# The value product of attention with its high and low part in one matmul

## Chip, cores and metric

One core of a Trainium2 chip. The metric is the device time of one execution in microseconds: 647.28 as the median of 3 runs of the kernel before (647.21 to 647.37). Inputs and output are float32.

## What is computed

One decoder block on 1024 tokens of width 1024: an RMS norm, one input projection, two groups of heads side by side, and an output projection with a residual and a final norm. The group that the change touches is stick-breaking attention with 8 heads of 64 dimensions:

```
for blk in range(t_len // BLOCK_Q):              # 8 blocks of 128 queries
    z = einsum('bhqd,bhkd->bhqk', qb, kb) * scale
    sp = where(causal, softplus(z), 0.0)
    tail = cumsum(sp, reverse=True) - sp
    attn = where(causal, exp(log_sigmoid(z) - tail), 0.0)
    outs.append(einsum('bhqk,bhkd->bhqd', attn, vb))
```

The other group is a gated delta rule in chunks (4 heads of 128), which the text calls delta. Both end in a norm per head and a gate, and then in `x + mixed @ w_out`.

## The kernel before

**Precision.** Most products are made from float32 values split in two: a high part, which a copy to the type float32r makes, and a low part, the rest, which a subtraction gives. A projection is three matmuls (high by high, high by low, low by high; `mm3`, L586). The values v are kept as both parts beside each other in one tile v2a, 64 columns each, so that one load of 128 weight columns holds both. The attention weights are split too, into tiles ah and al.

**An order written by a planner.** Every operation is first recorded with a cost by hand (`cost`, L393) in a model of the engines (`Model`, L169), and issued by streams (generators) that yield when they must wait. `interleave` (L440) always takes the stream of the lowest number that can go on: delta before attention, then the steps of the output, and as filling (number 100 and above) the projections and the output products. What the model finds fixes the order of all engines (L1574 to L1577), and on the chip each engine keeps that order and waits by semaphores. A record's line in the profile is therefore always L358; operations are told apart by their tiles. A changed cost or wait anywhere gives a new order everywhere behind it.

**Attention.** For every head, four windows of two query blocks each (`window`, L1291): scores in PSUM banks pz, two sigmoids on ScalarE, a scan on VectorE (cc) and a product on GpSimd (tile sg). Then, with tile st over the same memory, groups j of key blocks are transposed on TensorE (L1329), copied to ah by ScalarE and subtracted to al by VectorE (L1332, L1333). The value product follows one group behind (L1349 to L1353): for each key block s two matmuls, one from ah and one from al, add into columns 0 to 255 of bank po. They are 256 columns wide (two query blocks), and 128 wide for the last key block of a window, which only the second query block sees. ScalarE copies the sum to o2 (L1358), TensorE transposes it, VectorE adds the two halves of 64 rows (oe), and a DMA stores it. ah and al have two buffers each.

**Other users of these buffers.** They also hold two column halves of q before the store (`q_evac`, L597), the blocks of v before the store (`v_evac`, L723, tile v2e, four buffers in all, eight blocks early and eight in `values`, L770), and a small tile cs of the decays (L819).

**The end.** When delta is done, the output weights 4 to 7 are loaded (tile wor) and split (woh, wol); the block inputs (mgf) are loaded, scaled, transposed (matmuls into pz from step and mwf) and split (mh, ml). Output products (pp from woh or wol and mh or ml) run when the projections are used up.

Of the kernel before, what the change touches and what calls it, by code (L numbers as in the profile page):

```python
# [10 lines left out]
F32 = mybir.dt.float32  # L11
F32R = mybir.dt.float32r
I32 = mybir.dt.int32
AF = mybir.ActivationFunctionType
ALU = mybir.AluOpType
AX = mybir.AxisListType

P = 128
# [5 lines left out]
SBD = 64  # L24
# [449 lines left out]
def block(tc, xT_d, x_d, n1_d, wE_d, wQ_d, wC_d, conv_d, alog_d, dtb_d, mixw_d, wo_d, fnw_d, out_d):  # L474
    nc = tc.nc
    ck = Model({"V": nc.vector, "A": nc.scalar, "G": nc.gpsimd, "P": nc.tensor, "S": nc.sync})
    V, A, G, TE, S = ck.V, ck.A, ck.G, ck.P, ck.S

    with ExitStack() as top:
# [60 lines left out]
        at_ = open_pool("att", side="right")  # L540
        proj_ctx = top.enter_context(ExitStack())
        pr = open_pool("pr", side="right")
# [4 lines left out]
        s0 = open_pool("s0", ctx=s0_ctx)  # L547
# [49 lines left out]
        def q_evac(pt, i, half):  # L597
            hs = slice(half * 512, (half + 1) * 512)
            j = 2 * i + half
            apart = j in (1, 3, 5)  # L600
            if apart:
                pool, tags, bufs = ((at_, ("ah", "al"), 2), (pr, ("kt", "kt"), 2))[j % 4 // 2]
                hi, lo = [pool.tile([P, 512], F32R, tag=tag, bufs=bufs, name="xq") for tag in tags]
            else:
                t = s0.tile([P, 2, 512], F32R, tag="xr", bufs=5, name="xq")
                hi, lo = t[:, 0, :], t[:, 1, :]
            A.activation(hi, pt, AF.Copy)
            V.tensor_tensor(lo, pt, hi.bitcast(F32), ALU.subtract)
            ck.prio, prio = 1, ck.prio
            if apart:  # L610
                later(S.dma_start(qk_s[i, 0, :, hs].bitcast(F32), hi.bitcast(F32)), scale)
                later(S.dma_start(qk_s[i, 1, :, hs].bitcast(F32), lo.bitcast(F32)), scale)
            else:
                later(S.dma_start(qk_s[i, :, :, hs].rearrange("a p t -> p a t").bitcast(F32), t.bitcast(F32)), scale)
            ck.prio = prio
# [102 lines left out]
        def first(f, *args, bank=BANK, **kw):  # L718
            ck.prio, prio = bank, ck.prio
            f(*args, **kw)  # L720
            ck.prio = prio

        def v_evac(pt, b, col, h0, scale):  # L723
            src = pt[:, col:col + 256].rearrange("p (h d) -> p h d", d=SBD)
            v2 = at_.tile([P, 4, 2, SBD], F32R, tag=("al", "ah")[b % 2], bufs=2, name="v2e")
            A.activation(v2[:, :, 0, :], src, AF.Copy, scale=scale)
            V.scalar_tensor_tensor(v2[:, :, 1, :], src, scale, v2[:, :, 0, :].bitcast(F32), ALU.mult, ALU.subtract)
            S.dma_start(v_s[b, :, h0:h0 + 4, :, :].bitcast(F32), v2.bitcast(F32))

        early = Columns(8)  # L730
        early.load()
# [51 lines left out]
        def decays(me):  # L783
            n32 = GH * NB
            V.tensor_tensor(xg, ga[:, :, 4:8].rearrange("p c h -> p h c"), dtb.unsqueeze(2).to_broadcast([P, GH, NB]), ALU.add)
            V.scalar_tensor_tensor(ab, xg, -1.0, xg, ALU.mult, ALU.max)
            A.activation(ug, ab, AF.Exp, scale=-1.0)
            A.activation(ea, alog, AF.Exp)
            V.tensor_scalar(y1, ug, 2.0, None, ALU.add)
            V.reciprocal(y1, y1)  # L790
            V.tensor_tensor(y1, y1, ug, ALU.mult)
            V.tensor_tensor(y2, y1, y1, ALU.mult)
            V.tensor_scalar(hn, y2, 1.0 / 17.0, 1.0 / 15.0, ALU.mult, ALU.add)
            for c in (13.0, 11.0, 9.0, 7.0, 5.0, 3.0, 1.0):
                V.tensor_tensor(hn, hn, y2, ALU.mult)
                V.tensor_scalar(hn, hn, 1.0 / c, None, ALU.add)
            V.tensor_tensor(hn, hn, y1, ALU.mult)
            V.tensor_scalar(xg, xg, 0.0, None, ALU.max)
            V.scalar_tensor_tensor(hn, hn, 2.0, xg, ALU.mult, ALU.add)
            r = V.scalar_tensor_tensor(hn, hn, -1.0, ea.unsqueeze(2).to_broadcast([P, GH, NB]), ALU.mult, ALU.mult)  # L800
            hf = hn.rearrange("p h c -> p (h c)")
            yield r
            gp = pz()
            TE.matmul(gp[:, 0:n32], triu, hf, start=True, stop=True)
            TE.matmul(gp[:, n32:2 * n32], ones, hf, start=True, stop=True)
            cum = gsc["cum"]
            fl = lambda t: t.rearrange("p h c -> p (h c)")
            V.tensor_copy(fl(cum), gp[:, 0:n32])
            V.tensor_copy(gl, gp[:, n32:2 * n32])
            A.activation(fl(gsc["eg"]), fl(cum), AF.Exp)  # L810
            A.activation(fl(gsc["egl"]), gl, AF.Exp)
            V.tensor_tensor(gl, gl, fl(cum), ALU.subtract)
            V.tensor_scalar(gl, gl, 0.0, None, ALU.min)
            A.activation(fl(gsc["kd"]), gl, AF.Exp)
            yield V.tensor_scalar(gsc["neg"], gsc["eg"], -1.0, None, ALU.mult)
            ct = pz()
            TE.transpose(ct[0:n32, 0:P], fl(cum), ident)
            TE.transpose(ct[0:n32, P:2 * P], fl(gsc["eg"]), ident)
            cs = at_.tile([P, 2 * P], F32, tag="al", bufs=2, name="cs")  # L819
            V.tensor_copy(cs[0:n32], ct[0:n32, 0:2 * P])  # L820
            S.dma_start(cum_s.rearrange("a h c j -> (h c) a j"), cs[0:n32].rearrange("p (a j) -> p a j", a=2))
            yield

            me.other = DECAYS
            for h in range(GH):
                for g in range(2):
                    hc = slice(4 * g, 4 * g + 4)
                    dt = gd.tile([P, 4, P], F32, tag=("kn", "at", "nkv")[(2 * h + g) % 3], bufs=4, name="dt")
                    S.dma_start(dt, cum_s[0, h, hc].partition_broadcast(P))
                    G.tensor_tensor(dt, dt, cum[:, h, hc].unsqueeze(2).to_broadcast([P, 4, P]), ALU.subtract)  # L830
                    G.affine_select(dt, dt, pattern=[[0, 4], [1, P]], compare_op=ALU.is_ge, fill=-1e4, base=0, channel_multiplier=-1)
                    A.activation(dt, dt, AF.Exp)
                    S.dma_start(dt_s[h, g], dt)
                    yield
            A.activation(gsc["beta"], ga[:, :, 0:4].rearrange("p c h -> p h c"), AF.Sigmoid)
            me.other = DELTA + 0.7
            flags["dec"] = True
# [453 lines left out]
        def window(h, w, tok):  # L1291
# [3 lines left out]
            for i in range(2):  # L1295
                b = 2 * w + i
# [25 lines left out]
            for j in range(w + 2):  # L1322
                if j <= w:
                    yield lambda: busy["al"] < 2
                    busy["al"] += 1
                    blocks = [(s, i) for s in (2 * j, 2 * j + 1) for i in range(2) if s <= 2 * w + i]
                    n = len(blocks)
                    tp = pz()
                    yield from turned(tp, [st[:, i, s * P:(s + 1) * P] for s, i in blocks])  # L1329
                    ah = at_.tile([P, 512], F32R, tag="ah", bufs=2, name="ah")  # L1330
                    al = at_.tile([P, 512], F32R, tag="al", bufs=2, name="al")
                    A.activation(ah[:, 0:n * P], tp[:, 0:n * P], AF.Copy)  # L1332
                    r = V.tensor_tensor(al[:, 0:n * P], tp[:, 0:n * P], ah[:, 0:n * P].bitcast(F32), ALU.subtract)  # L1333
                    if j == w:
                        busy["T"] = 0
                        busy[tok] = 0
                    parts.append((ah, al, r))
                    yield
                if j == 0:
                    continue  # L1340
                if j == 1:
                    yield lambda: busy["po"] == 0
                    busy["po"] = 1
                    ov = po()
                    yield from until(f"va{h}")
                    v2 = hd["v", h]
                ah, al, r = parts[j - 1]
                yield r
                for s in (2 * (j - 1), 2 * (j - 1) + 1):  # L1349
                    i0 = 0 if s <= 2 * w else 1  # L1350
                    c = slice(256 * (s % 2), 256 * (s % 2) + (1 if i0 else 2) * P)
                    for m, t in enumerate((ah, al)):
                        TE.matmul(ov[:, i0 * P:256], v2[:, s, :], t[:, c], start=(s == 0 and m == 0), stop=(s == 2 * w + 1 and m == 1))  # L1353
                busy["al"] -= 1
                if j < w + 1:
                    yield
            o2 = fx.tile([P, 256], F32, "o2", "o2")
            yield A.activation(o2, ov[:, 0:256], AF.Copy)  # L1358
            busy["po"] = 0
            op = pz()  # L1360
            ot = fx.words(o2, "ot")
# [249 lines left out]
```

## Time and profile before

| | |
|---|---|
| median of 3 runs | 647.28 us |
| span of the profiled execution, first to last instruction | 644.7 us |
| TensorE, share of the span | 99% |
| VectorE, ScalarE, GpSimd | 67%, 61%, 53% |
| matmuls in the trace | 3976 |
| of these into bank po from ah and al | 320 |

The profile is of one execution; its span leaves out some 2.6 us of what the timed runs contain. In the timeline the columns are start, duration, engine, line, operation, output<-inputs, shape and count. PE is the matmul side of TensorE, PEld its weight loads. Shapes of matmuls are given as weights, then partitions by columns of the moving operand.

### The profile page before, as it was taken

The numbers are of one execution on the slowest core, as the hardware profiler recorded it, in microseconds if no ns is written. First come the engines' busy times: TensorE is split into PE (matmuls) and PEld (weight loads), VectorE is DVE, ScalarE is ACT, GpSimd is POOL, SyncE is SP. The second block draws the span as 40 slices with busy tenths as digits, with TensorE's granted clock in tenths as the row PEclk, the third lists the DMA queues.
The fourth block names the chain that finished last, engine by engine and source line by source line (L and its number), as shares of the span: only waits on it lengthen the run. The fifth ranks groups of instructions, "written<-read, shape, count | busy, mean of one in ns | idle before, by whom it ended". The sixth has DMA issues, their size and how long they took to land.

```text
span 644.7 us, 11693 instructions
## 1 busy us (share of the span) xinstructions
PE 635.5 (99%) x3976; PEld 551.4 (86%) x3976; DVE 430.3 (67%) x778; ACT 392.8 (61%) x943; POOL 340.5 (53%) x429
## 2 busy tenths in 40 slices
PE   8999999999999999999999999999999999999996
PEld 7889989988888889898889888889888988888885
DVE  4469984233776786875686767677678736468864
ACT  5664566633876686767676874686679642133553
POOL 0115143864979494855587783677445242136532
PEclk9999999999999999999999999999999999999998
DMA  8886244886267244448236583164342279773222
GB/s 301 317 286 243 89 145 148 321 277 229 82 201 255 89 162 131 148 111 254 81 107 186 159 246 126 68 168 141 100 146 68 87 261 322 261 228 99 67 112 116
DMA packets 96666, 111.82 MB, mean 173 GB/s; under 512 B 28576, under 2 KB 61536, under 8 KB 96608
## 3 DMA queue, kind: packets, MB, share of 16 engines
q1 hardware_dynamic: 96320, 110.89, 52.8%
q8 instruction: 31, 0.51, 0.3%
q14 instruction: 27, 0.22, 0.1%
q10 hardware_dynamic: 288, 0.20, 0.1%
HBM read 76.03 MB, written 35.03 MB: 172 GB/s over the span
## 4 chain that ended last, share of the span: by engine, by line
PE 90%; DVE 3%; POOL 3%; issue 1%; ACT 1%; DMA 1%; SPq 0%; POOLq 0%; DVEq 0%; ACTq 0%
PE pp L358 52%; PE pz L358 27%; PE po L358 8%; PE pc L358 3%; DMA dt<-cum_s 1%; DVE cc L358 1%; POOL wel L358 1%; POOL rsb L358 1%; SPq L358 0%; POOL tm L358 0%; DVE ssb L358 0%; POOL ac L358 0%; POOL xs L358 0%; DVE mgf L358 0%; ACT sgf L358 0%
## 5 line engine op out<-in xcount | busy, mean ns | idle before, releaser
L358 PE MATMUL pp<-xh,weh 128*128 128x512 f32 x360 | 146.0, 405 | 0.0
L358 PE MATMUL pp<-xh,wel 128*128 128x512 f32 x360 | 141.2, 392 | 0.0
L358 PE MATMUL pp<-xl,weh 128*128 128x512 f32 x360 | 140.5, 390 | 0.0
L358 POOL TENSOR_TENSOR wel<-wer,weh 128x512 fp32r<-128x512 f32 x48 | 63.1, 1317 | 68.2 <-ACT weh L358 66.5
L358 POOL TENSOR_TENSOR sgf<-sgf,cc 128x128 f32<-128x128 f32 (+3 forms) x64 | 77.0, 1208 | 39.8 <-DVE cc L358 32.5
L358 PEld LDWEIGHTS pp<-xh,wel 128*128 128x128 f32 x360 | 67.6, 188 | 15.2
L358 PEld LDWEIGHTS pp<-xl,weh 128*128 128x128 f32 x360 | 67.7, 188 | 11.7
L358 PEld LDWEIGHTS pp<-xh,weh 128*128 128x128 f32 x360 | 67.5, 188 | 11.6
L358 DVE TENSOR_TENSOR_SCAN cc<-pz,step 128x384 f32<-128x384 f32 (+2 forms) x64 | 53.6, 849 | 15.7 <-ACT pz L358 10.4
L358 DVE TENSOR_TENSOR al<-pz,ah 128x512 fp32r<-128x512 f32 (+1 forms) x80 | 49.9, 631 | 19.0 <-ACT ah L358 18.6
L358 ACT ACTIVATE ah<-pz 128x512 fp32r<-128x512 f32 (+1 forms) x80 | 43.9, 563 | 21.6 <-PE pz L358 21.2
L358 ACT ACTIVATE sgf<-pz,rs 128x384 f32<-128x384 f32 (+3 forms) x96 | 53.4, 589 | 3.3 <-PE pz L358 2.6
L358 ACT ACTIVATE pz<-pz,ns 128x384 f32<-128x384 f32 (+3 forms) x96 | 52.4, 570 | 0.1
L358 PE MATMUL pp<-woh,mh 128*128 128x512 f32 (+2 forms) x132 | 51.8, 392 | 0.1
L358 PE MATMUL pp<-woh,ml 128*128 128x512 f32 (+2 forms) x132 | 50.9, 385 | 0.0
L358 PE MATMUL pp<-wol,mh 128*128 128x512 f32 (+2 forms) x132 | 50.6, 384 | 0.0
L358 POOL TENSOR_TENSOR ac<-ac,pre 128x512 f32<-128x512 f32 x24 | 30.9, 1288 | 29.2 <-ACT pre L358 17.2
L358 DVE SCALAR_TENSOR_TENSOR pp<-pre,conv,pp 128x512 f32<-128x512 f32 x42 | 31.5, 751 | 18.2 <-ACT pp L358 17.6
L358 POOL TENSOR_TENSOR ml<-mf,mh 128x512 fp32r<-128x512 f32 x16 | 21.5, 1345 | 41.8 <-ACT mh L358 37.4
L358 PE MATMUL po<-ah,v2a 128*128 128x256 f32 (+1 forms) x160 | 43.1, 296 | 0.0
L358 DVE TENSOR_TENSOR_SCAN cc<-pz,cc,step 128x512 f32<-128x512 f32 (+1 forms) x32 | 38.7, 1211 | 4.0 <-ACT pz L358 2.8
L358 PE MATMUL po<-al,v2a 128*128 128x256 f32 (+1 forms) x160 | 38.7, 280 | 0.0
(291 smaller groups left out, 1590.0 us busy)
## 6 DMA issues: line engine op xcount, KB each, us to landing
wer<-wE SPq DMA_DIRECT2D x48, 256.0 KB, 3.5
xr<-x SPq DMA_DIRECT2D x16, 512.0 KB, 7.1
g_s<-ac SPq DMA_DIRECT2D x24, 256.0 KB, 2.3
v_s<-v2e SPq DMA_DIRECT2D x16, 256.0 KB, 2.7
kqf<-g_s SPq DMA_DIRECT2D x16, 256.0 KB, 3.6
v2a<-v_s SPq DMA_DIRECT2D x8, 512.0 KB, 5.1
q<-qk_s SPq DMA_DIRECT2D x8, 512.0 KB, 4.6
kh<-qk_s SPq DMA_DIRECT2D x8, 512.0 KB, 4.8
```

Of the source, the lines that this page charges most:

```text
L358: ins = f(*args, **kw).ins
```

## The change

ah and al become the two halves of one tile ahl (same size in all, two buffers). For each key block one matmul takes both: its moving operand is two runs of columns of ahl, 512 columns apart, and its output goes to two halves of bank po, the high part's sum in columns 0 to 255 and the low part's in 256 to 511. With two query blocks that is 512 columns, with one it is two runs of 128. After the last key block ScalarE copies the first half to o2, as before, and VectorE adds the second half to it. The other users of the buffers follow: two blocks of v share one buffer, which is held until the second is issued; two of the column halves of q lie in one buffer and are stored by one DMA; cs takes a whole buffer.

```
-                    ah = at_.tile([P, 512], F32R, tag="ah", bufs=2, name="ah")
-                    al = at_.tile([P, 512], F32R, tag="al", bufs=2, name="al")
+                    ahl = at_.tile([P, 2, 512], F32R, tag="ahl", bufs=2, name="ahl")
+                    ah, al = ahl[:, 0, :], ahl[:, 1, :]
...
-                    for m, t in enumerate((ah, al)):
-                        TE.matmul(ov[:, i0 * P:256], v2[:, s, :], t[:, c], start=(s == 0 and m == 0), stop=(s == 2 * w + 1 and m == 1))
+                    TE.matmul(ov2[:, :, i0 * P:256], v2[:, s, :], ahl[:, :, c], start=s == 0, stop=s == 2 * w + 1)
...
-            yield A.activation(o2, ov[:, 0:256], AF.Copy)
+            A.activation(o2, ov[:, 0:256], AF.Copy)
+            yield V.tensor_tensor(o2, ov[:, 256:512], o2, ALU.add)
...
-            v2 = at_.tile([P, 4, 2, SBD], F32R, tag=("al", "ah")[b % 2], bufs=2, name="v2e")
+            if b % 2 == 0:
+                v2p[0] = at_.tile([P, 2, 4, 2, SBD], F32R, tag="ahl", bufs=2, name="v2e")
+                ck.hold(v2p[0])
+            v2 = v2p[0][:, b % 2]
...
-                hi, lo = [pool.tile([P, 512], F32R, tag=tag, bufs=bufs, name="xq") for tag in tags]
+                hi, lo = [pr.tile([P, 512], F32R, tag="kt", bufs=2, name="xq") for _ in range(2)]
...
+                t = at_.tile([P, 2, 512], F32R, tag="ahl", bufs=2, name="xq") if j in (1, 5) else s0.tile([P, 2, 512], F32R, tag="xr", bufs=5, name="xq")
...
-            cs = at_.tile([P, 2 * P], F32, tag="al", bufs=2, name="cs")
+            cs = at_.tile([P, 8 * P], F32, tag="ahl", bufs=2, name="cs")[:, 0:2 * P]
```

How it moves the instructions, at two places. First TensorE in the first window of the first head: v2a are the values, stf the weights to be transposed, kh and kl the keys. Before:

```order
L358 MATMUL pp<-xh,wel 128x512
L358 MATMUL po<-ah,v2a 128x256
L358 MATMUL po<-al,v2a 128x256
L358 MATMUL po<-ah,v2a 128x128
L358 MATMUL po<-al,v2a 128x128
L358 MATMUL pz<-step,stf_1958 128x128 x7
L358 MATMUL pz<-kh,q_1701 128x512
```

TensorE at the same place, now:

```order
L358 MATMUL pp<-xh,wel 128x512
L358 MATMUL po<-ahl,v2a 128x512
L358 MATMUL po<-ahl,v2a 128x2x128
L358 MATMUL pz<-step,stf_1944 128x128 x7
L358 MATMUL pz<-kh,q_1689 128x512
```

Four matmuls have become two, with the same neighbours. Further on the orders drift apart. The second place is TensorE at the last product of delta (pz from vr and at). Before:

```order
L358 MATMUL pz<-state,kqf_4761 128x128
L358 MATMUL pz<-vr,at 128x128
L358 MATMUL po<-ah,v2a 128x256
L358 MATMUL po<-al,v2a 128x256
L358 MATMUL po<-ah,v2a 128x256
L358 MATMUL po<-al,v2a 128x256
L358 MATMUL pz<-step,stf_6662 128x128 x3
L358 MATMUL pp<-xh,weh 128x512
```

TensorE at the last product of delta, now:

```order
L358 MATMUL pz<-state,kqf_4742 128x128
L358 MATMUL pz<-vr,at 128x128
L358 MATMUL pp<-xh,weh 128x512
L358 MATMUL pp<-xl,weh 128x512
L358 MATMUL pp<-xh,wel 128x512
L358 MATMUL pp<-xh,weh 128x512
```

Attention, whose last value products stood behind the end of delta, is now done before it, and behind it there are only projections. From this row to the first output product (pp from woh and mh) there were 40 groups of three projection matmuls, and 25 to the first transposes of a block input (mwf); now there are 32 and 27.

More of the change, by code (lines that the diff above doesn't have):

```diff
@@ L599, in q_evac @@
             j = 2 * i + half
-            apart = j in (1, 3, 5)
+            apart = j == 3
             if apart:
-                pool, tags, bufs = ((at_, ("ah", "al"), 2), (pr, ("kt", "kt"), 2))[j % 4 // 2]
-                hi, lo = [pool.tile([P, 512], F32R, tag=tag, bufs=bufs, name="xq") for tag in tags]
+                hi, lo = [pr.tile([P, 512], F32R, tag="kt", bufs=2, name="xq") for _ in range(2)]
             else:
-                t = s0.tile([P, 2, 512], F32R, tag="xr", bufs=5, name="xq")
+                t = at_.tile([P, 2, 512], F32R, tag="ahl", bufs=2, name="xq") if j in (1, 5) else s0.tile([P, 2, 512], F32R, tag="xr", bufs=5, name="xq")
                 hi, lo = t[:, 0, :], t[:, 1, :]
@@ L721, in first @@
             ck.prio = prio
+        v2p = [None]
         def v_evac(pt, b, col, h0, scale):
             src = pt[:, col:col + 256].rearrange("p (h d) -> p h d", d=SBD)
-            v2 = at_.tile([P, 4, 2, SBD], F32R, tag=("al", "ah")[b % 2], bufs=2, name="v2e")
+            if b % 2 == 0:
+                v2p[0] = at_.tile([P, 2, 4, 2, SBD], F32R, tag="ahl", bufs=2, name="v2e")
+                ck.hold(v2p[0])
+            v2 = v2p[0][:, b % 2]
             A.activation(v2[:, :, 0, :], src, AF.Copy, scale=scale)
@@ L728, in v_evac @@
             S.dma_start(v_s[b, :, h0:h0 + 4, :, :].bitcast(F32), v2.bitcast(F32))
+            if b % 2:
+                ck.free(v2p[0])
         early = Columns(8)
@@ L1336, in window @@
                         busy[tok] = 0
-                    parts.append((ah, al, r))
+                    parts.append((ahl, r))
                     yield
@@ L1346, in window @@
                     v2 = hd["v", h]
-                ah, al, r = parts[j - 1]
+                ahl, r = parts[j - 1]
+                ov2 = ov.rearrange("p (m t) -> p m t", m=2)
                 yield r
```

## Prediction

> **What bounds the kernel now.** I read the page's busy shares and its chain first, then TensorE's waits, then the timeline around the products that change.
>
> ```profile
> PE 635.5 (99%) x3976; PEld 551.4 (86%) x3976; DVE 430.3 (67%) x778; ACT 392.8 (61%) x943; POOL 340.5 (53%) x429
> PEclk9999999999999999999999999999999999999998
> PE 90%; DVE 3%; POOL 3%; issue 1%; ACT 1%; DMA 1%; SPq 0%; POOLq 0%; DVEq 0%; ACTq 0%
> PE po L358 <- DVE step L358: 1.7, 1, 1.7
> PE pp L358 <- DVE v2e L358: 0.6, 1, 0.6
> PE pz L358 <- DVE oe L358: 0.2, 1, 0.2
> ```
>
> TensorE is busy for 99% of the 644.7 us span at an unthrottled clock, and 90% of the chain that ended last runs over it. The last three rows are all the waits of TensorE that the trace names: 2.5 us. The planner fills TensorE with projection and output products whenever attention has nothing ready, so a microsecond taken out of the TensorE stream anywhere should come out of the end, if no new wait takes its place. The other engines matter only where they make TensorE wait.
>
> A matmul's duration does not price it: matmuls overlap, and a 512-column one is given 0.39 us though the next begins 0.23 us later. The price is the distance from one start to the next. The first window's value product, in the timeline of TensorE, shows every size that I need:
>
> ```profile
> 172.51 0.40 PE L358 MATMUL pp<-xh,wel 128*128 128x512 f32 x1
> 172.74 0.28 PE L358 MATMUL po<-ah,v2a 128*128 128x256 f32 x1
> 172.86 0.28 PE L358 MATMUL po<-al,v2a 128*128 128x256 f32 x1
> 172.98 0.22 PE L358 MATMUL po<-ah,v2a 128*128 128x128 f32 x1
> 173.04 0.28 PE L358 MATMUL po<-al,v2a 128*128 128x128 f32 x1
> 173.16 0.25 PE L358 MATMUL pz<-step,stf 128*128 128x128 f32 x1
> ```
>
> 512 columns cost 0.23 (172.51 to 172.74). 256 columns cost 0.12 each, so a high and low pair costs 0.24 (172.74 to 172.98). A pair of 128 columns costs not half of that but 0.18 (172.98 to 173.16): the high part takes 0.06 and the low part 0.12. So a matmul of 128 columns behind a like one begins no sooner after it than one of 256 would let the next begin; both load 128 weight columns, and I take that load to be what it waits for. Longer runs give the third digit, each shown by its first row and the row behind its last:
>
> ```profile
> 77.81 0.39 PE L358 MATMUL pz<-xh,weh 128*128 128x512 f32 x1
> ...
> 83.25 0.39 PE L358 MATMUL pp<-xh,weh 128*128 128x512 f32 x1
> ```
>
> ```profile
> 516.76 0.28 PE L358 MATMUL po<-ah,v2a 128*128 128x256 f32 x1
> ...
> 517.23 0.39 PE L358 MATMUL pp<-xh,weh 128*128 128x512 f32 x1
> ```
>
> 24 matmuls of 512 columns take 5.44, or 0.2267 each; two wide pairs take 0.47, or 0.235 a pair.
>
> **The change part by part.** How many pairs there are of each size, from the groups by form:
>
> ```profile
> L358 PE MATMUL po<-ah,v2a 128*128 128x256 f32 x128 | 37.5, 314 | 0.0
> L358 PE MATMUL po<-al,v2a 128*128 128x256 f32 x128 | 33.2, 281 | 0.0
> L358 PE MATMUL po<-al,v2a 128*128 128x128 f32 x32 | 8.8, 276 | 0.0
> L358 PE MATMUL po<-ah,v2a 128*128 128x128 f32 x32 | 7.1, 222 | 0.0
> ```
>
> *The wide pairs.* 128 pairs of 256 columns become 128 matmuls of 512. The same number of columns goes through, so only the fixed part of one instruction goes. 0.235 - 0.2267 = 0.0083, and 128 x 0.0083 = 1.1 us.
>
> *The narrow pairs.* 32 pairs of 128 columns become 32 matmuls of 256. The pair costs 0.18 above and 0.17 in the rows below (489.39 to 489.56), so 0.175, against 0.12: 32 x 0.055 = 1.75 us. This is the larger half although it is a fifth of the pairs.
>
> *What follows a narrow pair.* Two runs of three transposes, both followed by a full-fp32 product (the trace has two matmuls for each of these in the order, and I call them two-pass):
>
> ```profile
> 486.36 0.37 PE L358 MATMUL pz<-step,stf 128*128 128x128 f32 x3
> 486.56 0.46 PE L358 MATMUL pz<-v,kn 128*128 128x128 f32 x2
> ...
> 489.39 0.22 PE L358 MATMUL po<-ah,v2a 128*128 128x128 f32 x1
> 489.45 0.28 PE L358 MATMUL po<-al,v2a 128*128 128x128 f32 x1
> 489.56 0.42 PE L358 MATMUL pz<-step,stf 128*128 128x128 f32 x3
> 489.82 0.46 PE L358 MATMUL pc<-xct,xinv 128*128 128x128 f32 x2
> ```
>
> Behind a wide pair the three take 0.20, behind a narrow one 0.26. In the order of the program 21 narrow pairs stand right before transposes. Between nothing and 21 x 0.06 = 1.3 us is gained; I take 0.5, since the next operation takes up some of it. TensorE's stream thus shortens by 1.1 + 1.75 + 0.5 = 3.3 us.
>
> *Added.* One addition per window on VectorE, 32 in all, reading 256 columns of PSUM and 256 of SBUF. The nearest row:
>
> ```profile
> L358 DVE TENSOR_TENSOR at<-pz,dt 128x256 f32<-128x256 f32 x16 | 6.4, 415 | 3.4 <-PE pz L358 3.4
> ```
>
> 32 x 0.415 = 13.3 us on an engine with a third of its time free. It comes after the copy on ScalarE and before the transposes of the window's output, so bank po stays taken about 0.5 us longer per window. The 32 windows' value products lie between 172.74 and some microseconds behind 516.76, one every 11 us, so po is free by then. Queued behind the addition on VectorE are the next window's low parts, the scans and the delta chain's xct, v and state. TensorE has projections to do meanwhile, so this costs nothing as long as there are projections: cover gone, the bound is 32 x 0.415 = 13 us.
>
> *Buffers.* ah and al share one buffer of the same size, and a value product already waited for the later of them. The value blocks that are written out early now share a buffer two by two, so the fifth block waits for the store of the second, not of the first alone:
>
> ```profile
> 115.76 0.51 SPq L358 DMA_DIRECT2D v_s<-v2e  x1
> 123.79 0.36 ACT L358 ACTIVATE v2e<-pp 128x256 fp32r<-128x256 f32 x1
> DMA to landing us min/median/max: 2.0/2.7/6.2
> ```
>
> In the second half of the values the second block's store is issued at 115.76 and lands by 122.0 at the longest; the fifth block is written at 123.79. Nothing is added. Two stores of q become one instead of two, on a queue that TensorE does not wait for there: nothing.
>
> *Moved.* The planner lays out all engines anew. By the order of TensorE, what changes at a place that can hurt is the end of the delta rule. Its last product must go through the norm, a store and load, a scaling, transposes and a split before the first output product, and projections cover this:
>
> ```profile
> 514.38 0.28 PE L358 MATMUL pz<-vr,at 128*128 128x128 f32 x1
> 528.91 0.88 DVE L358 TENSOR_SCALAR mgf<-mgf,rsg 128x128 f32<-128x128 f32 x4
> 533.59 0.46 PE L358 MATMUL pz<-step,mwf 128*128 128x128 f32 x4
> 536.61 1.54 POOL L358 TENSOR_TENSOR ml<-mf,mh 128x512 fp32r<-128x512 f32 x1 [4.39 <-DMA xr<-x]
> 545.01 0.39 PE L358 MATMUL pp<-woh,mh 128*128 128x512 f32 x1
> ```
>
> Now ml is ready at 538.15 and used at 545.01: 6.9 us to spare. Before, 40 groups of three projection matmuls lie between the last delta product and the first output product; after, 32, that is 96 x 0.2267 = 21.8 us, plus 0.4 for one set of transposes: 22.2. The same chain took 538.15 - 514.38 = 23.8 us, which would make TensorE wait 1.6 us. But the scaled block was there at 529.8 and its transposes stood 3.8 us later in the order; after, they stand at 81 x 0.2267 = 18.4 us behind the last delta product, 0.8 earlier. So the wait lies between 0 and 1.6; I take 0.5, as the inputs were early.
>
> **Sum.** -3.3 + 0.5 = -2.8 us. The span of 644.7 goes to 641.9. The median run is 647.28, 2.6 above the span of the profiled one; that part (start and end of the program) the change does not touch. 641.9 + 2.6 = 644.5 us. Ends of the terms: -1.1 - 1.75 - 1.3 = -4.2 at best (643.1) and -1.1 - 1.75 + 1.6 = -1.2 at worst (646.1).
>
> **The rivals.**
>
> *The gain is spent at the end of the delta rule (or another wait of that size).* The planner's new order leaves the first output product no reserve. If loads of the output weights or the block inputs land 1.5 us later than before, TensorE idles 1.6 + 1.5 = 3.1 us with no projection left to fill it: 647.3 - 3.3 + 3.1 = 647.1. For it: the missing 8 groups. Against it: the scaled block waited 3.8 us. Chance 0.18.
>
> *The new operand form is slow, and the kernel slower.* The moving operand is now two runs of columns 512 apart, and in 32 matmuls the output too is two runs of 128 in the bank with 128 between. No row of this trace has such a matmul in single pass. The slowest pace that the trace has for 256 columns is that of the two-pass products:
>
> ```profile
> 308.03 1.89 PE L358 MATMUL pz<-kqf 128*128 128x256 f32 x8
> 309.76 0.38 PE L358 MATMUL pc<-xct,xinv 128*128 128x128 f32 x2
> ```
>
> 1.73 / 8 = 0.216 each. At that pace the 128 would cost 0.432 instead of 0.235 and the 32 0.216 instead of 0.175: 25.2 + 1.3 = 26.5 us more, 673.8. If only the 32 with a split output are hit, they lose 1.3 and the others win 1.1: 647.5. With the 32 as forecast, the change is slower from the point where a wide matmul takes over 0.235 + (1.3 + 1.75) / 128 = 0.259. The Trainium skill, in PSUM — Partial Sum Buffer, Specifications (TRN2), says that "any non-contiguous AP slows matmuls significantly"; by that rule at least the 32 would pay, and no row here shows it. I hold against it that the runs are 128 and 256 columns long, so that a matmul meets one jump. Chance of the whole 0.07.
>
> *The stream shrinks by more.* All terms come out at their best, and the two waits of TensorE for VectorE that the first fence shows behind a value block and behind an attention output (0.6 and 0.2) fall away in the new order: 4.2 + 0.8 = 5.0 us, 642.3. For it: the order is new there. Against it: most waits are already gone. Chance 0.12.
>
> *Replanning costs more than the stream gains*, somewhere that I do not see, by at least the 3.3 us gained and 1.3 more (648.6 and over): chance 0.03.
>
> **How the numbers follow.** A run of this kernel can be told from no change from about 0.2%, 1.3 us, on. The forecast (643.1 to 646.0) has 0.60, the larger gain 0.12, the spent gain 0.18, slow operands 0.07, replanning 0.03. Faster: 0.60 + 0.12 = 0.72. Same: 0.18. Slower: 0.10. The range goes from the larger gain, 642.3, to 646.9, most of the way into the spent gain; the slow cases and the rest of the spent gain stay outside.
>
> **What would show it.** Right: a group po<-ahl of 160 matmuls with next starts at 0.23 and 0.12; TensorE's last start about 3 us earlier; TensorE's waits still under 4 us in all; the additions on VectorE near 0.4 us. Wrong: starts behind po<-ahl over 0.26 apart; a wait of TensorE for ml, woh or wol near 535 us; a wait for al's successor in the windows; a lower clock row.

## The result and the profile after

The changed kernel takes 645.85 us as the median of 14 runs (645.63 to 646.11), against 647.34 of 14 runs of the kernel before beside it, one of which took 878.74 us. The ratio is 0.9978 with a 95% interval of 0.9970 to 0.9986, so the change gains 1.5 us (0.9 to 1.9) where 2.8 were forecast. The spans of the two profiled executions are 643.7 and 644.7 us.

Of the page: the engines' busy time, and then all the waits of TensorE that the trace names (total, how often, the longest).

```profile
PE 633.7 (98%) x3816; PEld 540.5 (84%) x3816; DVE 436.0 (68%) x810; ACT 392.8 (61%) x943; POOL 340.3 (53%) x429
```

```profile
PE po L358 <- DVE step L358: 1.7, 1, 1.7
PE pp L358 <- DVE xr L358: 1.2, 2, 0.8
PE pz L358 <- DVE cc L358: 0.5, 2, 0.3
```

160 matmuls fewer, 32 operations of VectorE more. The first wait, at the start, was there before. The waits for v2e and oe (0.6 and 0.2 us before) are gone; a wait for xr, an operation of the output stage, is new.

The new matmuls and the new addition among the groups by form, and the first window in TensorE's timeline:

```profile
L358 PE MATMUL po<-ahl,v2a 128*128 128x512 f32 x128 | 45.2, 431 | 0.0
L358 PE MATMUL po<-ahl,v2a 128*128 128x256 f32 x32 | 9.0, 281 | 0.0
L358 DVE TENSOR_TENSOR o2f<-po,o2f 128x256 f32<-128x256 f32 x32 | 13.4, 420 | 8.9 <-ACT o2f L358 8.7
```

```profile
172.79 0.40 PE L358 MATMUL pp<-xh,wel 128*128 128x512 f32 x1
173.03 0.52 PE L358 MATMUL po<-ahl,v2a 128*128 128x512 f32 x2
173.38 0.72 PE L358 MATMUL pz<-step,stf 128*128 128x128 f32 x7
```

The row with x2 holds a wide and a narrow matmul. They take 0.35 us (173.03 to 173.38), where the two pairs took 0.42 (172.74 to 173.16). The addition takes 0.420 us, as its nearest row had said (0.415).

To see where the time went I took for each matmul the distance from its start to the next one's start, and summed these by kind:

| us | before | after |
|---|---|---|
| value products, wide (128) | 34.55 | 34.42 |
| value products, narrow (32) | 5.57 | 3.91 |
| transposes stf | 25.26 | 23.44 |
| projection of the values | 47.25 | 46.42 |
| output products | 88.98 | 90.84 |
| all, from the first matmul's start to the last's | 636.36 | 635.39 |

The first four kinds lose 4.4 us, more than the 3.3 forecast for the stream; 0.8 of this is in the projection of the values, with the wait for v2e gone, and need not be the change's (see e8). The output products take 1.9 us more. There the new wait lies. TensorE after, from the first output product on; first the row of that product, then what stands around the gap, then a second wait for xr:

```profile
541.82 0.39 PE L358 MATMUL pp<-woh,mh 128*128 128x512 f32 x1
...
545.11 0.39 PE L358 MATMUL pp<-woh,ml 128*128 128x512 f32 x1
546.28 0.50 PE L358 MATMUL pp<-woh,mh 128*128 128x512 f32 x1 [0.78 <-DVE xr L358]
...
601.61 0.39 PE L358 MATMUL pp<-woh,ml 128*128 128x512 f32 x1
602.42 0.47 PE L358 MATMUL pp<-woh,mh 128*128 128x512 f32 x1 [0.42 <-DVE xr L358]
```

Starts of 512 columns are otherwise 0.23 apart, so the gaps cost 546.28 - 545.11 - 0.23 = 0.94 and 602.42 - 601.61 - 0.23 = 0.58: 1.5 us. Who holds TensorE up at 545 is seen on GpSimd, ScalarE and VectorE of the same stretch:

```profile
540.00 1.55 POOL L358 TENSOR_TENSOR ml<-mf,mh 128x512 fp32r<-128x512 f32 x1 [10.16 <-DMA mgf<-og_s]
```

```profile
542.08 0.60 ACT L358 ACTIVATE zs<-pp 128x512 f32<-128x512 f32 x1 [2.21 <-PE pp L358]
```

```profile
545.54 0.69 DVE L358 TENSOR_TENSOR xr<-pp,xr 128x512 f32<-128x512 f32 x1 [1.08 <-PE pp L358]
546.51 0.69 DVE L358 TENSOR_TENSOR mf<-pz,mgf 128x512 f32<-128x512 f32 x1 [0.28 <-POOL ml L358]
547.12 0.68 DVE L358 TENSOR_TENSOR zt<-pp,zs 128x512 f32<-128x512 f32 x1
```

Bank pp has two buffers. One holds the last projection, a gate: ScalarE has made its sigmoid zs by 542.68, but the product zt, which frees the bank, stands behind xr and mf on VectorE and comes at 547.12. The other holds the first output product, which xr frees at 546.2. TensorE wants a third and waits. Before, the zt of the last gate (the second zt below) stood ahead of the first xr on VectorE:

```profile
542.27 0.69 DVE L358 TENSOR_TENSOR mf<-pz,mgf 128x512 f32<-128x512 f32 x1 [2.07 <-POOL ml L358]
542.88 0.68 DVE L358 TENSOR_TENSOR zt<-pp,zs 128x512 f32<-128x512 f32 x1
545.89 0.69 DVE L358 TENSOR_TENSOR zt<-pp,zs 128x512 f32<-128x512 f32 x1 [2.33 <-ACT zs L358]
...
547.95 0.69 DVE L358 TENSOR_TENSOR xr<-pp,xr 128x512 f32<-128x512 f32 x1 [0.59 <-PE pp L358]
```

The second gap, at 602, has another cause. VectorE had worked without a pause since 597.3, on norms and an mf, and came to the xr that frees the bank only then:

```profile
601.59 0.68 DVE L358 TENSOR_TENSOR xr<-pp,xr 128x512 f32<-128x512 f32 x1
```

The two profiles also start differently, and that is not the change's. The first 670 matmuls are the same in both kernels, yet the 28th starts at 8.33 before and at 9.47 after:

```profile
8.33 0.39 PE L358 MATMUL pc<-xh,wqh 128*128 128x512 f32 x1
```

```profile
6.98 0.63 PE L358 MATMUL pp<-xl,wqh 128*128 128x512 f32 x1
7.41 0.60 PE L358 MATMUL pz<-xl,wqh 128*128 128x512 f32 x1
...
9.47 0.39 PE L358 MATMUL pc<-xh,wqh 128*128 128x512 f32 x1
```

Of the 1.14 us, 0.43 is there already at the first projection (4.68 and 5.11). Then projections of 512 columns start 0.43 apart (6.98 to 7.41), and from a certain moment on 0.23. That moment falls differently in each execution: in the 14 profiled ones of this study the 28th matmul starts between 8.33 and 9.63. From the 28th to the last matmul (638.03 before, 637.06 after) it is 629.70 and 627.59, 2.1 us less. But most of the early start was lost again in the wait for v2e: the 661st matmul, behind that wait and ahead of the first value product, starts at 119.58 before and at 119.83 after. From there to the last matmul it is 518.45 and 517.23, 1.2 us less, and this goes better with the 1.5 of the timed runs.

### The profile page after: what moved, and what is told of

It is laid out like the page before. It is cut to its first block, busy times and chain, and to the rows that moved or that the text cites. A ratio compares the mean times of both kernels' runs of the same rounds, so it can differ in the third digit from the quotient of the medians.

```text
span 643.7 us, 11378 instructions
## 1 busy us (share of the span) xinstructions
PE 633.7 (98%) x3816; PEld 540.5 (84%) x3816; DVE 436.0 (68%) x810; ACT 392.8 (61%) x943; POOL 340.3 (53%) x429
## 4 chain that ended last, share of the span: by engine, by line
PE 54%; POOL 3%; issue 2%; DVE 1%; POOLq 0%; ACT 0%
PE pp L358 34%; PE pz L358 14%; PE po L358 4%; PE pc L358 2%; POOL sgf L358 1%; POOL rsb L358 1%; POOL tt L358 0%; DVE xr L358 0%; POOL ac L358 0%; DVE cc L358 0%; POOL wel L358 0%; POOL ml L358 0%; POOL ry L358 0%; DVE ssb L358 0%; DVE ac L358 0%
## 5 line engine op out<-in xcount | busy, mean ns | idle before, releaser
L358 DVE TENSOR_TENSOR ahl<-pz,ahl 128x512 fp32r<-128x512 f32 (+1 forms) x80 | 50.1, 632 | 12.3 <-ACT ahl L358 11.9
L358 ACT ACTIVATE ahl<-pz 128x512 fp32r<-128x512 f32 (+1 forms) x80 | 44.1, 564 | 17.7 <-PE pz L358 17.4
L358 PE MATMUL po<-ahl,v2a 128*128 128x512 f32 (+1 forms) x160 | 49.0, 401 | 0.0
L358 PE MATMUL pz<-kh,q 128*128 128x384 f32 (+3 forms) x96 | 36.1, 382 | 0.2 <-DVE cc L358 0.2
```

Of the source, the lines that this page charges most:

```text
L358: ins = f(*args, **kw).ins
```

## The experiments

The theory after the result: the narrow pairs give most of the gain, the wide ones nearly nothing, and half of it is lost at the end, through the order that the planner made of the additional operation. The rivals: the jump in the operands costs something and eats the gain of the wide pairs; or VectorE's 13 us more cost TensorE time in any order. All runs but e9 to e12 keep the planner's constants. Each ratio is to runs of the kernel before on the same chip; their median was 647.33 beside e1 to e4, 647.40 beside e5 to e8, 647.10 beside e9 to e11 and 646.54 beside e12.

### Layout without jumps (e1)

The two parts lie beside each other for each block of 128 queries, so that the moving operand and the output of every value product are one run of columns.

```
-    ahl = at_.tile([P, 2, 512], F32R, tag="ahl", bufs=2, name="ahl")
-    ah, al = ahl[:, 0, :], ahl[:, 1, :]
+    ahl = at_.tile([P, 4, 2, P], F32R, tag="ahl", bufs=2, name="ahl")
+    ah, al = ahl[:, 0:n, 0, :], ahl[:, 0:n, 1, :]
...
-    ov2 = ov.rearrange("p (m t) -> p m t", m=2)
+    ov2 = ov.rearrange("p (i m t) -> p i m t", i=2, m=2)
```

> The changed kernel with ahl laid out so that the moving operand and the output of every value product are one run of columns (high and low part of a query block side by side); ScalarE and VectorE then write and read runs of 128 columns. The order of all engines is that of the changed kernel. Theory A (two runs of columns cost a matmul nothing; a wide one costs 0.233 instead of the 0.227 of the forecast because all matmuls of 512 do so among attention's other work): 645.9 us, starts behind a wide product still 0.233 apart. Rival B (the jump in the operand costs 6 ns, in the split output more): 128 x 0.006 = 0.8 us less, 645.1, and 0.227 apart. Rival C (runs of 128 slow the copy and the subtraction): each ahl copy over its 0.56 us, time above 646.2.

Measured: 645.98 us, ratio 0.9983 (0.9974 to 0.9991), the time of the changed kernel. The value products sum to 38.32 us (38.33 in the changed kernel). The first window's wide and narrow matmul again take 0.36 together:

```profile
173.11 0.52 PE L358 MATMUL po<-ahl,v2a 128*128 128x512 f32 x2
173.47 0.72 PE L358 MATMUL pz<-step,stf 128*128 128x128 f32 x7
```

So the jump in operand and output costs nothing that can be seen. Only the 32 narrow ones have an output in two runs; they sum to 3.91 us in the changed kernel and 3.90 in e1. The rule of the Trainium skill that the prediction weighed (PSUM — Partial Sum Buffer, Specifications (TRN2)) is not borne out here for runs of 128 float32 columns.

### Merged matmuls taken apart again (e2, e3, e4)

In the changed kernel's own order, merged matmuls are issued as two again: all but the first key block's (32 narrow, 96 wide; e2), the 96 wide alone (e3), the 32 narrow alone (e4). The planner sees one operation as before, so that nothing else moves.

```
+    if name == "matmul" and self.model.split and self.model.split(args[2]):
+        f(args[0][:, 0, :], args[1], args[2][:, 0, :], start=False, stop=False)
+        ins = f(args[0][:, 1, :], args[1], args[2][:, 1, :], start=False, stop=kw["stop"]).ins
+    else:
+        ins = f(*args, **kw).ins
...
+    ck.split = lambda t: s > 0                          # e2
+    ck.split = lambda t: s > 0 and t.shape[2] == 256    # e3
+    ck.split = lambda t: t.shape[2] == 128              # e4
```

> The changed kernel, in its own order of all engines, with 128 of the 160 merged matmuls issued as two again (all 32 narrow ones and 96 wide ones; the first of a window stays merged, as it opens both halves of the bank). Everything else, the added addition and the buffers too, stays. Theory A (the gain of the change is the narrow pairs and the transposes behind them): 96 x 0.0025 + 32 x 0.052 + 1.0 to 1.8 for the transposes = 2.9 to 3.7 us more than the changed kernel, 648.8 to 649.6, so over the kernel before, since addition, buffers and new order together cost some 1.5 to 2. Rival B (the new order brought the gain, the matmuls little): 646 to 646.8.

> The changed kernel, in its own order, with only the 96 wide products behind the first of a window issued as two again. Theory A (a wide pair costs 0.236, a merged one 0.2335): 96 x 0.0025 = 0.2 us more, 646.1, not to be told from the changed kernel. Rival B (the forecast's 0.0083 each): 0.8 us more, 646.7.

> The changed kernel, in its own order, with only the 32 narrow products issued as two again. Theory A (the narrow pairs with the transposes behind them are the gain): 1.7 + 1.0 to 1.8 = 2.7 to 3.5 us more, 648.6 to 649.4. Rival B (only the pairs themselves count, the transposes catch up): 1.7 us more, 647.6. Rival C (the wide ones are the gain): under 0.5 us more.

Measured, and the two kinds of matmul from each trace:

| | us | ratio (95%) | value products | transposes stf |
|---|---|---|---|---|
| changed kernel | 645.85 | 0.9978 (0.9970 to 0.9986) | 38.33 | 23.44 |
| e3, wide apart | 646.16 | 0.9982 (0.9973 to 0.9991) | 38.59 | 23.43 |
| e4, narrow apart | 648.11 | 1.0013 (1.0004 to 1.0022) | 39.92 | 24.36 |
| e2, both apart | 648.39 | 1.0017 (1.0008 to 1.0026) | 40.26 | 24.41 |

By the medians the wide pairs gave 0.3 us and the narrow ones 2.25. The 0.3 is within the noise of the medians (e1 and the changed kernel differ by 0.13, and the intervals overlap), but the value products of e3's trace take 0.26 more. By the traces the narrow ones gave 1.6 in the products themselves and 0.9 in the transposes behind them. In the first window of e4 the narrow pair is back to 0.06 and 0.11 (L360 and L361 are the two halves), while the wide matmul ahead of it takes 0.24:

```profile
173.14 0.40 PE L363 MATMUL po<-ahl,v2a 128*128 128x512 f32 x1
173.38 0.22 PE L360 MATMUL po<-ahl,v2a 128*128 128x128 f32 x1
173.44 0.28 PE L361 MATMUL po<-ahl,v2a 128*128 128x128 f32 x1
173.55 0.77 PE L363 MATMUL pz<-step,stf 128*128 128x128 f32 x7
```

And e2, which has the addition, the buffers and the order of the change but hardly its matmuls, is 1.1 us slower than the kernel before: the rest of the change costs time.

### Buffers alone, addition alone (e8, e7)

e8 is the kernel before with ahl and its other users' buffers, and still 320 matmuls. e7 is the kernel before with one operation of VectorE more per window, a maximum of o2 and the bank that o2 was copied from.

```
+    yield V.tensor_tensor(o2, ov[:, 0:256], o2, ALU.max)    # e7
```

> The kernel with only the buffers of the change (one tile ahl, two value blocks and two halves of q in a buffer, cs in a whole one), with the 320 matmuls of the kernel before into 256 columns and without the addition. Theory A: nothing, 647.0 to 647.5; the wait for v2e near 118 us (0.6) may come or go. Rival B (the shared value buffers make TensorE wait in the values): over 648.

> The kernel before, with its 320 matmuls and its buffers, and one more operation of VectorE per window between the copy to o2 and the transposes: the maximum of bank po and o2, which leaves o2 as it is. Theory A (the addition costs nothing by itself, but as it stands in the way of delta's chain on VectorE the end of delta comes later against the projections, here too: 116 rows instead of 138 from the last product of delta to the first output product): 0.8 to 1.4 us more, 648.1 to 648.7, with waits for xr near 545 us. Rival B (the new order of the changed kernel comes from the shorter matmuls or the buffers): 647.3.

e8: 646.66 us, ratio 0.9987 (0.9978 to 0.9996). By the medians the buffers alone gain about 0.7. The projection of the values takes 46.41 instead of 47.25, and the wait for v2e is gone; but that the new buffers end it is not shown: e7, and e6 below, have the old buffers, and their traces have no such wait either (46.40 in e6, 46.39 in e7). With the old buffers it stands in three of five traces, with the new ones in none of nine. And from the 661st matmul to the last, e8 takes 518.42 us, as before (518.45). e7: 650.11 us, 1.0040 (1.0027 to 1.0052): 2.7 us slower. More than all of that is in the output stage: from the first output product to the last matmul it is 96.2 us, before 93.0. Of its waits of TensorE, beside the old one at the start, the largest are these:

```profile
PE pz L358 <- issue: 1.1, 1, 1.1
PE pp L358 <- DVE xr L358: 1.0, 2, 0.8
```

Issue stands for a wait whose cause the trace does not name. The addition alone brings the wait for xr. That it acts through the order and not through its own 13 us was still a reading.

### A mend by the stores of the gates (e5, e6)

The stores of the last two gates got the priority of the output weights, in the changed kernel (e5) and in the kernel before (e6), to bring zt ahead of xr.

```
-    return S.dma_start(gate_s[i, :, hs], zt)
+    ck.prio, prio = (OUT_WEIGHTS if i > 1 and i < 4 else ck.prio), ck.prio
+    r = S.dma_start(gate_s[i, :, hs], zt)
+    ck.prio = prio
+    return r
```

> The changed kernel, where the stores of the last projections' gates (z2 and z3) go ahead of the output's loads on the DMA queue of SyncE, so that the buffer of the last gate zt is free in time and VectorE empties the last projection's bank pp before the first output addition xr. TensorE's order up to the first output product stays. Theory A (the two waits of TensorE for xr near 545 us, 0.8 and 0.4, are a cost of the new order that only the late zt makes): 1.2 us less than the changed kernel, 644.7, and no wait for xr. Rival B (the first output products wait for the split ml or for wol instead): 645.5 to 646.

> The kernel before with the same stores ahead. Theory A: it has no wait for xr at the end, so nothing changes, 647.3. Rival B (the earlier stores are worth something by themselves): 646.5 or less.

The mend failed. e6: 646.88 us, 0.9991 (0.9983 to 1.0000), nothing or a little faster. e5: 649.79 us, 1.0039 (1.0026 to 1.0051). The wait for xr at 545 is gone, but the planner laid out the rest anew, and further on mh and ml come late:

```profile
588.14 0.39 PE L358 MATMUL pp<-woh,ml 128*128 128x512 f32 x1
589.15 0.52 PE L358 MATMUL pz<-step,mwf 128*128 128x128 f32 x4 [0.63 <-PE pp L358]
591.69 0.50 PE L358 MATMUL pp<-woh,mh 128*128 128x512 f32 x1 [2.02 <-ACT mh L358]
...
593.39 0.80 PE L358 MATMUL pp<-woh,ml 128*128 128x512 f32 x1 [0.97 <-POOL ml L358]
```

The waits are 3.6 us, and from 592.4 on, as the third begins, TensorE's clock is halved for some 7 us (the stretch 593 to 599 of it: busy time and count of each engine, then the granted clock):

```profile
593.00:599.00 6.00, 5.61 (x16) 4.44 (x17) 3.88 (x7) 1.89 (x3) 3.26 (x3) 0.50 0.36 98
```

### Another order by the planner's slack (e9, e10, e11)

A stream of the planner may go on when, by the model, the result that it waits for has been there for SLACK ns (L437). A smaller value gives another order of the same instructions. With 350 the order of the changed kernel has 114 projection matmuls between the last product of delta and the first output product (96 with 450, 120 before the change), and zt ahead of xr again.

```
-SLACK = 450
+SLACK = 350    # e9, on the changed kernel; e10 has 400; e11 has 350 on the kernel before
```

> The changed kernel with one constant of the planner smaller (SLACK 450 to 350), which gives another order of the same instructions: 114 matmuls of projections instead of 96 stand between the last transposed block of delta and the first output product, and the last gate's zt stands ahead of the first xr on VectorE again, as before the change. Theory A (the addition costs nothing itself; the order that it brought costs about 1.2 to 1.9 us at the end of delta, through the wait for the first xr): the wait at the start of the output stage is gone and the time is 644.0 to 644.7 us, 1.2 to 1.9 below the changed kernel's 645.85. Rival B (a smaller slack takes reserve from other places, so TensorE waits there instead): 645.9 us or more, with new waits of TensorE of over 1 us in sum. Rival C (the wait is not in the order but in VectorE's extra 13 us): the wait for xr stays, 645.5 to 646.2 us.

> The changed kernel with SLACK 400: only 90 matmuls of projections stand ahead of the first output product (96 with 450), but the last gate's zt stands ahead of the first xr on VectorE. Tells apart what of the order counts. Theory A (zt behind xr holds the bank of pp): no wait for xr, 644.3 to 645.2 us, with a wait for ml of at most 0.5 us. Rival (the reserve, the number of projections ahead of the first output product, counts): a wait for ml or mh of 1 us or more at the start of the output stage, 645.9 to 647 us.

> The kernel before with SLACK 350: the control for what the constant does by itself. Theory A (the constant helps the changed kernel only by mending the order that the change brought): 646.9 to 648.0 us, as before or a little above (102 matmuls of projections ahead of the first output product instead of 120). Rival (a smaller slack is better for either kernel): 646.3 us or less.

e9: 644.21 us (643.95 to 644.35), ratio 0.9954 (0.9942 to 0.9967), as theory A had it, 1.6 below the changed kernel (0.9978 - 0.9954 = 0.0024 of 647 us). TensorE's waits, and VectorE and TensorE at the place in question:

```profile
PE po L358 <- DVE step L358: 1.7, 1, 1.7
PE pp L358 <- POOL wel L358: 0.3, 1, 0.3
```

```profile
541.03 0.69 DVE L358 TENSOR_TENSOR mf<-pz,mgf 128x512 f32<-128x512 f32 x1 [2.07 <-POOL ml L358]
541.64 0.68 DVE L358 TENSOR_TENSOR zt<-pp,zs 128x512 f32<-128x512 f32 x1
543.82 0.69 DVE L358 TENSOR_TENSOR zt<-pp,zs 128x512 f32<-128x512 f32 x1 [1.50 <-ACT zs L358]
...
545.88 0.69 DVE L358 TENSOR_TENSOR xr<-pp,xr 128x512 f32<-128x512 f32 x1 [0.59 <-PE pp L358]
```

```profile
542.94 0.39 PE L358 MATMUL pp<-woh,mh 128*128 128x512 f32 x1
...
635.61 0.28 PE L358 MATMUL pp<-woh,ml 128*128 128x192 f32 x1
```

Both zt are through before the first xr, the wait is gone, and the output stage takes 635.61 - 542.94 = 92.7 us: no longer than before (638.03 - 545.01 = 93.0). e9 has all 32 additions too (13.3 us of VectorE), and behind the start no wait of TensorE for VectorE of over 0.2 us. So the 13 us do not cost TensorE time in every order.

e11, the control, is 647.77 us, 1.0010 (1.0001 to 1.0019): the constant by itself gains nothing. It has a wait of its own, 1.6 us for mh ahead of its first output product, and without it would stand near 646.1, a little below the kernel before. So of the 3.6 us between e11 and e9 that wait is 1.6; the other 2 are what merged matmuls, buffers, addition and another order give together.

e10 is 645.35 us, 0.9973 (0.9962 to 0.9983), above theory A's 645.2 and without the wait for ml that the rival wanted. TensorE waits for zt itself there:

```profile
545.79 0.39 PE L358 MATMUL pp<-woh,ml 128*128 128x512 f32 x1
546.95 0.50 PE L358 MATMUL pp<-woh,mh 128*128 128x512 f32 x1 [0.77 <-DVE zt L358]
```

```profile
545.61 0.69 DVE L358 TENSOR_TENSOR mf<-pz,mgf 128x512 f32<-128x512 f32 x1 [2.54 <-POOL ml L358]
546.21 0.68 DVE L358 TENSOR_TENSOR zt<-pp,zs 128x512 f32<-128x512 f32 x1
```

zt is ahead of the first xr, as it should be, and still late, because mf ahead of it on VectorE waits 2.54 us for GpSimd's ml. So zt against xr is not all that counts. TensorE waits where an operation that frees a bank pp stands in VectorE's queue behind one that cannot start: behind xr, which waits for the first output product to end, in the changed kernel, and behind mf, which waits for GpSimd, in e10 (and in e7, where mf ahead of xr and zt waits 2.60 us).

### The addition alone, in another order (e12)

The kernel of e7 with SLACK 300, whose order has 123 projection matmuls ahead of the first output product and zt ahead of xr.

> The kernel before with one operation of VectorE more per window (as e7), and SLACK 300, which gives that kernel an order with a reserve of 123 matmuls of projections ahead of the first output product and the last gate's zt ahead of the first xr on VectorE. It lacks the merged matmuls, so only what the addition costs is left in it. Theory A (the addition itself costs nothing, the order that it brought did): 646.9 to 648.0 us, the time of the kernel before within about 0.5 us either way, with no wait for xr or ml in the output stage of over 0.5 us. Rival (13 us more of VectorE cost TensorE something in any order): 649 us or more, as e7 with 650.1.

652.19 us, ratio 1.0084 (1.0070 to 1.0098): theory A's number missed by 4 us. TensorE again waits for a zt, this time with a projection, and VectorE shows why:

```profile
540.64 0.40 PE L358 MATMUL pp<-xh,wel 128*128 128x512 f32 x1
544.10 0.80 PE L358 MATMUL pp<-xh,weh 128*128 128x512 f32 x1 [3.07 <-DVE zt L358]
...
547.12 0.39 PE L358 MATMUL pp<-xl,weh 128*128 128x512 f32 x1
```

```profile
542.76 0.69 DVE L358 TENSOR_TENSOR mf<-pz,mgf 128x512 f32<-128x512 f32 x1 [2.03 <-POOL ml L358]
543.36 0.68 DVE L358 TENSOR_TENSOR zt<-pp,zs 128x512 f32<-128x512 f32 x1
```

```profile
544.00:547.00 3.00, 2.90 (x7) 2.35 (x8) 2.25 (x11) 0.71 (x2) 1.29 (x1) 0.51 0.87 251
```

It is the mechanism of e10 at a larger price: the gap costs 544.10 - 540.64 - 0.23 = 3.2 us, and at the granted clock of 0.51 behind it seven matmuls take 3.02 us (544.10 to 547.12) instead of 1.6, another 1.4. From the 661st to the last matmul e12 takes 523.62 us, 5.2 more than the kernel before; 4.6 of these (3.2 + 1.4) are that one place. The rest, with all 32 additions in it, takes about 0.5 us more by these two traces, and by the timed runs' interval (4.5 to 6.3 us slower) something between nothing and 1.7. So the rival's number came out, but for the most part not its reason: most of the cost lies at one place behind delta and not where the additions are.

## Why the prediction was right in sign and too large

By the steps of its sum:

- **Narrow pairs, -1.75 forecast.** Right. In the trace 5.57 us became 3.91, or -1.66, and taking the 32 apart again costs 2.25 us with the transposes behind them. That a narrow matmul waits for its weight load, as the prediction took it, no run tested.
- **Transposes behind them, -0.5 of 0 to 1.3.** Too small: 0.9 by e4. The trace of after has 1.8 less; the other 0.9 comes with the new order and was not taken apart further.
- **Wide pairs, -1.1.** Mis-sized: 0.3 by e3 for 96 of them, about 0.4 for all 128, and 0.1 between the two traces. The 0.235 of a pair was right (the median behind another single-pass product). The 0.2267 of the merged matmul was read from 24 projections in a quiet stretch; in its own place it takes 0.233, again the median. e1 shows that it is not the operands' form. What it is was not found.
- **The slow operand form.** Fell with e1.
- **Buffers, 0.** By the medians they gain about 0.7 (e8). The wait for v2e, which the prediction had only in a rival, fell away; whether the buffers did it is open, since e6 and e7 lack it with the old ones.
- **Addition, 0, "this costs nothing as long as there are projections".** This and the next are the steps that failed. In the windows it holds: the 13.4 us are hidden, since TensorE's waits name neither o2 nor the addition. But the planner, having one more operation to place, also lays out the end of delta anew: e7, the addition alone, is 2.7 us slower, with a wait for xr there.
- **End of delta, +0.5 of 0 to 1.6.** The place was right, the wait another one. ml is ready at 541.55 (540.00 + 1.55), 0.3 us ahead of the first output product at 541.82 where it was 6.9 ahead before, so the chain that the prediction followed is on time though its reserve is gone. TensorE waits instead for a bank of pp, 0.9 us at 545 and 0.6 at 602: 1.5 us.

By the experiments' medians the sum reads: buffers -0.7, narrow -2.25, wide -0.3, and, to reach the -1.5 measured, +1.75 for the addition with the order that it brings. This last term is what is left over, and each of the others carries an interval of 0.5 to 0.6 us either way; if the buffers gave nothing, it is 1.05. The two gaps in the trace, 1.5 us, lie within that. That e9 takes 1.6 us away by another order, with the same instructions, shows that a term of this size is the order's. Shown by rows is also the way it acts in e10 and e12 (mf waits for GpSimd, zt stands behind it, TensorE has no bank). Left open is how any one order could be known to be good without running it: SLACK 350 mended the changed kernel, 300 made e7's kernel worse, and with 350 the kernel before got a wait that it didn't have. The kernel before was tried with no other value, so what the change is worth between the best orders of both kernels is not known. The forecast's interval of 643.1 to 646.0 for its own case holds the result, but in part by luck, by errors that partly cancel: the transposes and perhaps the buffers gave more than forecast, the wide products less, and the end took more.

e9 is the fastest version here, 644.21 us.

## What to carry to other kernels

Count a narrow matmul by the measured distance to the next start, not by its columns: merging two of 128 columns saved 0.05 us each, six times what two of 256 would have by the most hopeful row. Where a planner sets the order, an operation that is hidden where it stands can still cost 1 to 5 us through the order that it brings. The number of projections kept in reserve was no guide: e12 had the most, 123, and lost the most. Look for the queue in which an operation that frees a bank can stand behind one that waits for another engine. When a change wins less than its parts, try another order of the same instructions before blaming the parts.

## What the runs showed of the hardware

- A moving operand of two runs of columns, 512 columns apart, and in 32 of them an output of two runs of 128, 256 apart, went at the pace of contiguous ones (38.33 us for the 160 matmuls, 38.32 in e1).
- A wait of TensorE of 3.07 us (e12) cost another 1.4 us behind it, where the granted clock was 0.51 for 3 us. Waits of 0.63, 2.02 and 0.97 us within 5 us (e5) came with a granted clock of 0.50 from 593 to 599, with matmuls of 512 columns 0.43 apart. Behind single waits of 0.8 (after) and 1.6 us (e11) the next matmuls were 0.23 apart again within a few steps. The Trainium skill (TensorE: Matmul & The Clock Gate, Part 1: The HAM clock gate) puts the halving behind an idle window of about 3.4 us that runs freely. Here a shorter idle time was enough: in the 3.4 us before the clock fell, TensorE was still busy for 0.90 us in e12 (540.13 to 543.54) and for 1.19 us in e5 (588.96 to 592.37).
- The first projections run at 0.43 us a matmul for a while that differs by execution (in after's until 7.8 us), though the granted clock of that stretch reads 1.00. Together with waits ahead of them this moves the 28th matmul by up to 1.3 us, but not the end of the profile by as much: of the 1.14 us between the two profiles 0.25 was left at the 661st.
